# Second attention of a two-layer trunk: TensorE's order written by hand

## The chip, the cores and the metric

One core of one Trainium2 chip runs the whole program. The metric is the device time of one execution in microseconds (us); of the kernel before, three runs took 2441.55, 2447.61 and 2448.34 us, so the median is 2447.61 us.

## The reference

Two decoder layers on 256 tokens of width 2048. The change touches the attention of the second layer, a stick-breaking attention with 16 heads of 128. Cut to what matters:

```python
q, k, v = jnp.split(h @ w_in, 3, axis=-1)          # 2048 -> 3 * 2048
z = jnp.einsum('bqhd,bshd->bhqs', qb, k) * scale
log_beta = jax.nn.log_sigmoid(z)
log_rest = jnp.where(strict, log_beta - z, 0.0)
later = lax.cumsum(log_rest, axis=3, reverse=True) - log_rest
weights = jnp.where(strict, jnp.exp(log_beta + later), 0.0)
o = jnp.einsum('bhqs,bshd->bqhd', weights, v)
y = o @ w_out                                       # 2048 -> 2048
```

## The kernel before

All weights are float32 in HBM. A **unit** of weights (`unit`, L329) is 512 rows by 512 columns: `fetch` (L98) loads it in two halves, ScalarE rounds each half to a high part `whi` and VectorE takes the low part `wlo` (`split`, L127 to L129), and TensorE multiplies both (L123 to L125, or L353 to L355). There are four buffers of each part, so two units can be ready or in use at a time. Each call of `unit` also ticks a **filler** (L310): it sums the adaLN weights of other parts of the model on VectorE (`add_row`, L205) and, at the end of each part, has TensorE do a little work. For a gate that is `gate_end` (L240), two products of a split sum with ones (L244, L245), which VectorE then multiplies into `gg` (L246), and the next quarter of the sum is split into `ahl`, which has one buffer (`gate_split`, L234). For columns it is `ada_columns` (L207), four transposes into `col` (L215) that VectorE sums (L216). A tick does 112/52 = 2.15 steps on the average in this stage (L963), and its steps are written before the unit's own products.

The second attention works on four groups of four heads (`hq` 0 to 3, L1047). `b_project(hq)` (L968) makes q, k and v of a group: four units for each, and it yields after each unit. `b_out(hq)` (L1032) multiplies a group's output with four units of `w_out` and yields after each. `b_attend(hq, pair)` (L997) does two heads, a **pair**: four products for the logits `z` of each head (L1006 to L1009), on ScalarE the absolute values (L1010), an Exp (L1012), a Ln after a table load (L1013), on VectorE `e` (L1015), then on TensorE the sums along the keys (L1016 to L1018), on ScalarE the Exp of the sums after another table load (L1021), and on TensorE the products with v into `bo` (L1024, L1025), which ScalarE and VectorE split into the two parts of `o` (L128, L129). Each sub-step of TensorE with float32 operands shows as two rows of the trace.

PSUM banks are handed out by rings. In this stage:

```python
banks(f=(0, 1), m=(2, 3), z=(4, 5, 7), s=(6,))     # L962
def small_ps(name, tag="s"): return bank(tag, name) # L153
```

The ring `s` has one bank, 6: `bo` of either head, `gate` and `col` all take it, so each waits until the one before it has been read. q and k use `f`, v and the units of `b_out` use `m`.

In which order the instructions of an engine stand is decided when the program is built: a scheduler takes, engine by engine, the earliest written instruction that it reckons ready, so it moves products of the units between the steps of a pair. The order is fixed once the program is built, and each engine works through its own in that order.

Of the kernel before, what the change touches and what calls it, by code (L numbers as in the profile page):

```python
# [12 lines left out]
AF = mybir.ActivationFunctionType  # L13
# [3 lines left out]
P = 128  # L17
# [26 lines left out]
def trunk(ctx: ExitStack, tc: tile.TileContext, x, c, rel_bias, ada_w, ada_b, norm_g, a_w_in, a_q_norm,  # L44
          a_kv_norm, a_idx_k_norm, a_w_qb, a_w_idx_qb, a_w_uk, a_w_uv, a_w_out, b_w_in, b_w_out,
          mlp_w1, mlp_w2, bucket, out):
    nc = tc.nc
# [7 lines left out]
    def uid(prefix, _n=[0]):  # L55
        _n[0] += 1
        return f"{prefix}_{_n[0]}"
# [12 lines left out]
                            fill=0.0, base=0, channel_multiplier=1)  # L70
# [5 lines left out]
                            fill=1.0, base=1 - P, channel_multiplier=1)  # L76
# [7 lines left out]
                            fill=-1.0, base=-1, channel_multiplier=-1)  # L84
# [34 lines left out]
    def rows(w, k0, k1, c0, c1):  # L119
        return w.rearrange("(a p) n -> p a n", p=P)[:, k0:k1, c0:c1]  # L120
# [6 lines left out]
    def split(dst_hi, dst_lo, src):  # L127
        return (nc.scalar.activation(dst_hi, src, AF.Copy).ins,  # L128
                nc.vector.tensor_sub(dst_lo, src, dst_hi.bitcast(F32)).ins)  # L129
# [18 lines left out]
    def bank(kind, name):  # L148
        ring = rings[kind]
        ring[1] += 1  # L150
        return psum.tile([P, BLK], F32, tag=f"bank{ring[0][(ring[1] - 1) % len(ring[0])]}", name=uid(name))

    def small_ps(name, tag="s"):  # L153
        return bank(tag, name)
# [174 lines left out]
    def unit(src, a, n, weight=1, into=None):  # L329
        if prepared:  # L330
            return prepared.pop()
        r = halves(fetch(src, a, n), a, n, into)
        filler.tick(weight)
        return r


    def s_piece(u, xk, nf, ps_tiles, n):

        for f in range(nf):
            o = ps_tiles[f // 2][:, (f % 2) * T:(f % 2 + 1) * T]  # L340
            fs = slice(f * P, (f + 1) * P)
            for k, hi, lo in u:
                xh, xl = xk(k)
                mm3(o, hi[:, fs], lo[:, fs], xh, xl, start=(k == 0 and f % 2 == 0), stop=(k == n - 1))

    def m_piece(u, xk, ps_tiles, n, tiles=range(NT)):

        for t in tiles:
            ts_ = slice(t * P, (t + 1) * P)
            o = ps_tiles[t]  # L350
            for k, hi, lo in u:
                xh, xl = xk(k)
                nc.tensor.matmul(o, xh[:, ts_], hi, start=(k == 0), stop=False)  # L353
                nc.tensor.matmul(o, xl[:, ts_], hi, start=False, stop=False)  # L354
                nc.tensor.matmul(o, xh[:, ts_], lo, start=False, stop=(k == n - 1))  # L355
# [121 lines left out]
    @contextmanager  # L477
    def quiet(what="hold"):

        with tc.issue_after(pace[what][0]), tc.issue_after(pace[what][1]):  # L480
            yield

    def pair_tile(i, name):

        return arena.tile([P, 2, 2, T], F32R, tag=f"slot{i}", name=uid(name))
# [11 lines left out]
    def first_products(ps_tiles, ws):  # L497

        for t in range(NT):
            for k, w in enumerate(ws):  # L500
                nc.tensor.matmul(ps_tiles[t], first32[t, k // 4][:, k % 4], w, start=(k == 0), stop=False)
# [83 lines left out]
    outs = ((pq, BLK, 0), (pk, W2, BLK))  # L585
    waiting = []
    for i in range(len(steps) + LEAD):
        if i < len(steps):
            start_load(i)
            g, k, _ = steps[i]  # L590
# [103 lines left out]
    for u in range(4):  # L694
# [7 lines left out]
        for a in range(2):  # L702
            qi = q_tile[:, u % 2, a].rearrange("p (a t) -> p a t", a=2)
            nc.scalar.activation(qi, pf[a].rearrange("p (a t) -> p a t", a=2), AF.Copy)
            for b in range(2):
# [7 lines left out]
                for t in range(NT):  # L713
                    o = score[:, rng[t][0]]
# [107 lines left out]
    for s in (slice(0, P), slice(2 * P, 3 * P)):  # L822
        nc.gpsimd.affine_select(out=score[:, s], in_=score[:, s], pattern=[[-1, P]], compare_op=ALU.is_ge,
                                fill=SENT, base=0, channel_multiplier=1)
    for t in range(NT):
        o = score[:, rng[t][0]]
# [5 lines left out]
    for s in (slice(0, P), slice(2 * P, 3 * P)):  # L832
        nc.gpsimd.affine_select(out=mask[:, s], in_=mask[:, s], pattern=[[-1, P]], compare_op=ALU.is_ge,
                                fill=-1.0, base=0, channel_multiplier=1)
# [133 lines left out]
    def b_project(hq):  # L968

        res = {}  # L970
        for part, tag in ((2, "v"), (0, "q"), (1, "k")) if hq == 0 else ((0, "q"), (1, "k"), (2, "v")):
            c0 = part * D + hq * BLK
            ps = [bank("m" if tag == "v" else "f", "p" + tag) for _ in range(2)]
            for u in range(4):
                first = hq == 0 and tag == "v"
                if first and u < 2:
                    if u == 0:
                        first_products(ps, early.pop("b"))
                    continue
                with quiet() if first else nullcontext():  # L980
                    prt = unit(rows(b_w_in[0], u * 4, u * 4 + 4, c0, c0 + BLK), 4, BLK)
                w = [(u * 4 + i, hi, lo) for i, (hi, lo) in enumerate(prt)]
                if tag == "v":
                    m_piece(w, hof, ps, NC)
                else:
                    s_piece(w, hof, 4, ps, NC)
                if u < 3:
                    yield
            both = arena.tile([P, 2, BLK], F32, tag=f"slot{12 + 2 * 'vkq'.index(tag) + hq % 2}", name=uid(tag))
            res[tag] = [both[:, i] for i in range(2)]  # L990
            for o, p_ in zip(res[tag], ps):
                nc.scalar.activation(o, p_, AF.Copy, scale=QS if tag == "q" else 1.0)
            yield
        projected[hq] = [[x_.rearrange("p (a t) -> p a t", a=2) for x_ in res["q"]],
                         [x_.rearrange("p (a t) -> p a t", a=2) for x_ in res["k"]], res["v"]]

    def b_attend(hq, pair):  # L997
        qT, kT, vt = projected[hq]
        kw = dict(skip_group_check=True)
        zs = []  # L1000
        both = arena.tile([P, 2, 3 * P], F32, tag=("slot18", "e")[pair[0] // 2], name=uid("e"))
        es = [both[:, i] for i in range(2)]
        for hl in pair:
            q_, k_ = qT[hl // 2][:, hl % 2], kT[hl // 2][:, hl % 2]
            z = small_ps("z", "z")
            nc.tensor.matmul(z[:, :T], k_[:, :P], q_, start=True, stop=False, **kw)  # L1006
            nc.tensor.matmul(z[:, T:3 * P], k_[:, P:], q_[:, P:], start=False, stop=False, **kw)
            nc.tensor.matmul(z[:, :P], big_ident, strict, start=False, stop=False, **kw)
            nc.tensor.matmul(z[:, T:3 * P], big_ident, strict, start=False, stop=True, **kw)  # L1009
            nc.scalar.activation(es[hl % 2], z[:, :3 * P], AF.Abs)  # L1010
            zs.append(z)
        nc.scalar.activation(both, both, AF.Exp, scale=-1.0)  # L1012
        nc.scalar.activation(both, both, AF.Ln, bias=1.0)  # L1013
        for z, e in zip(zs, es):
            nc.vector.scalar_tensor_tensor(e, z[:, :3 * P], 0.0, e, op0=ALU.max, op1=ALU.add)  # L1015
            nc.tensor.matmul(z[:, :T], neg_tri, e[:, :T], start=False, stop=False, **kw)  # L1016
            nc.tensor.matmul(z[:, P:T], neg_ones, e[:, T:], start=False, stop=False, **kw)
            nc.tensor.matmul(z[:, T:3 * P], neg_tri, e[:, T:], start=False, stop=True, **kw)  # L1018
        oo = pair_tile(8 + hq % 2 * 2 + pair[0] // 2, "o")
        for hl, (z, e) in enumerate(zip(zs, es), pair[0]):  # L1020
            nc.scalar.activation(e, z[:, :3 * P], AF.Exp)  # L1021
            po = small_ps("bo")
            hs = slice(hl * P, (hl + 1) * P)
            nc.tensor.matmul(po[:, :T], vt[0][:, hs], e[:, :T], start=True, stop=False, **kw)  # L1024
            nc.tensor.matmul(po[:, P:T], vt[1][:, hs], e[:, T:], start=False, stop=True, **kw)  # L1025
            o = oo[:, hl % 2]
            split(o[:, 0], o[:, 1], po[:, :T])
            o_tiles[hq].append(o)
# [3 lines left out]
    def b_out(hq):  # L1032
        for d in ((0,), (1,), (2,), (3,)) if hq < 3 else ((0,), (1, 2, 3)):
            kw = {}
            if d == (1, 2, 3):
                hts, ahead = next_h(mods[1, 4], mods[1, 3])
                handed.append(hts)
                kw = dict(early=lambda: load_mlp(1), ahead=ahead, hold=(12, 13, 14, 15))
            out_part(b_w_out[0], 4 * hq, 4, o_of(o_tiles[hq]), yt, gates.get((1, 2)), ss, d, hq == 0, hq == 3,
                     ("x", "f", "m")[-len(d):],  # L1040
                     **kw)
            yield

    yt, ss = new_y(ypool)
    for _ in b_project(0):
        pass
    for hq in range(4):  # L1047
        fill = []
        if hq > 0:
            fill.append((b_out(hq - 1), 2))  # L1050
        if hq < 3:
            fill.append((b_project(hq + 1), 6))
        for pair in ((0, 1), (2, 3)):
            b_attend(hq, pair)
            for gen, n in fill:
                for _ in range(n):
                    next(gen)
        for gen, _ in fill:
            for _ in gen:
                pass  # L1060
    filler.finish()
    for _ in b_out(3):
        pass
# [50 lines left out]
```

## Time and profile before

| what | value |
|---|---|
| median of 3 runs | 2447.61 us |
| the profiled execution | 2444.33 us |
| its span, first to last instruction | 2442.5 us |
| TensorE busy | 2350.5 us, 96% of the span |
| VectorE busy | 1747.2 us, 72% |
| ScalarE busy | 1222.3 us, 50% |
| from the first logits of the second attention to the first unit of `b_out(3)` | 1350.6 to 1678.4 us |

Busy time is the union of an engine's instructions. TensorE's products overlap, so one that is held up for a moment leaves less idle time in the trace than it lost; the distance between two starts tells more. The granted clock is given as a share of full speed: 1.00 is 2.4 GHz, 0.50 is 1.2 GHz.

### The profile page before, as it was taken

The numbers are of one execution on the slowest core, as the hardware profiler recorded it, in microseconds if no ns is written. First come the engines' busy times: TensorE is split into PE (matmuls) and PEld (weight loads), VectorE is DVE, ScalarE is ACT, GpSimd is POOL, SyncE is SP. The second block draws the span as 40 slices with busy tenths as digits, with TensorE's granted clock in tenths as the row PEclk, the third lists the DMA queues.
The fourth block names the chain that finished last, engine by engine and source line by source line (L and its number), as shares of the span: only waits on it lengthen the run. The fifth ranks groups of instructions, "written<-read, shape, count | busy, mean of one in ns | idle before, by whom it ended". The sixth has DMA issues, their size and how long they took to land.

```text
span 2442.5 us, 32827 instructions
## 1 busy us (share of the span) xinstructions
PE 2350.5 (96%) x12292; PEld 1957.9 (80%) x12292; DVE 1747.2 (72%) x2218; ACT 1222.3 (50%) x1825; POOL 41.0 (2%) x74
## 2 busy tenths in 40 slices
PE   5789999999999999999999999999999999999998
PEld 2478887868888888888878989987788888888886
DVE  6789798888576876876567678887855557655556
ACT  3056555566544544444455554456654454454443
POOL 0010000000000000000000000000000000000000
PEclk9799999999999999999999999999999999999999
DMA  9986789857677877877657779896666557656554
GB/s 371 346 311 233 267 307 309 292 206 267 232 261 246 293 269 274 303 253 272 193 186 257 239 264 328 304 335 221 235 239 191 185 188 263 216 189 190 182 189 146
DMA packets 281831, 613.93 MB, mean 251 GB/s; under 512 B 19668, under 2 KB 36392, under 8 KB 281160
## 3 DMA queue, kind: packets, MB, share of 16 engines
q1 hardware_dynamic: 278544, 603.14, 71.8%
q0 software_dynamic: 2464, 8.53, 1.2%
q8 instruction: 96, 1.57, 0.3%
q14 instruction: 63, 0.52, 0.1%
q10 hardware_dynamic: 664, 0.17, 0.0%
HBM read 609.62 MB, written 2.15 MB: 250 GB/s over the span
## 4 chain that ended last, share of the span: by engine, by line
PE 78%; DMA 7%; DVE 5%; ACT 4%; issue 4%; POOL 0%; SPq 0%; DVEq 0%; POOLq 0%; ACTq 0%
PE f L884 18%; PE m L355 11%; PE m L354 11%; PE m L353 11%; PE f L886 9%; DVE acc L205 2%; DMA raw<-in_a_w_out_dram 2%; DMA w<-in_ada_w_dram 2%; DMA adaw<-in_ada_w_dram 1%; ACT whi L128 1%; PE pv L353 1%; PE pv L354 1%; PE pv L355 1%; DVE wlo L129 1%; PE pq L123 1%
## 5 line engine op out<-in xcount | busy, mean ns | idle before, releaser
L129 DVE TENSOR_TENSOR wlo<-raw,whi 128x1024 fp32r<-128x1024 f32 x726 | 875.5, 1220 | 424.6 <-ACT whi L128 421.5
L128 ACT ACTIVATE whi<-raw 128x1024 fp32r<-128x1024 f32 x726 | 756.0, 1056 | 806.9 <-PE f L884 311.2
L884 PE MATMUL f<-h,whi 128*128 128x512 f32 x1920 | 675.9, 394 | 0.0
L886 PE MATMUL f<-h,wlo 128*128 128x256 f32 x1920 | 543.2, 283 | 0.2 <-DVE wlo L129 0.2
L884 PEld LDWEIGHTS f<-h,whi 128*128 128x128 f32 x1920 | 360.6, 188 | 82.5
L205 DVE SCALAR_TENSOR_TENSOR acc<-adaw,cs,acc 128x1024 f32<-128x1024 f32 x300 | 384.1, 1280 | 53.1 <-DMA adaw<-in_ada_w_dram 49.8
L353 PE MATMUL m<-whi,hid 128*128 128x512 f32 x1016 | 401.4, 395 | 0.0
L355 PE MATMUL m<-wlo,hid 128*128 128x512 f32 x1016 | 400.9, 395 | 0.0
L354 PE MATMUL m<-whi,hid 128*128 128x512 f32 x1016 | 400.9, 395 | 0.0
L886 PEld LDWEIGHTS f<-h,wlo 128*128 128x128 f32 x1920 | 360.9, 188 | 1.9 <-DVE wlo L129 0.8
L355 PEld LDWEIGHTS m<-wlo,hid 128*128 128x128 f32 x1016 | 191.3, 188 | 44.7
L353 PEld LDWEIGHTS m<-whi,hid 128*128 128x128 f32 x1016 | 191.4, 188 | 44.0
L354 PEld LDWEIGHTS m<-whi,hid 128*128 128x128 f32 x1016 | 191.4, 188 | 43.3
L387 DVE TENSOR_TENSOR y<-m,y 128x512 f32<-128x512 f32 x200 | 136.7, 685 | 38.4 <-PE m L355 38.0
L353 PE MATMUL m<-whi,o 128*128 128x512 f32 x368 | 149.8, 407 | 0.0
L355 PE MATMUL m<-wlo,o 128*128 128x512 f32 x368 | 146.5, 400 | 0.4 <-DVE wlo L129 0.4
L354 PE MATMUL m<-whi,o 128*128 128x512 f32 x368 | 146.8, 399 | 0.0
L205 DVE SCALAR_TENSOR_TENSOR acc<-w,cs,acc 128x1024 f32<-128x1024 f32 (+1 forms) x74 | 79.6, 1075 | 11.1 <-DMA w<-in_ada_w_dram 8.9
L355 PEld LDWEIGHTS m<-wlo,o 128*128 128x128 f32 x368 | 69.4, 189 | 15.6 <-DVE wlo L129 1.0
L353 PEld LDWEIGHTS m<-whi,o 128*128 128x128 f32 x368 | 69.6, 189 | 13.6 <-ACT qkv L754 0.2
L354 PEld LDWEIGHTS m<-whi,o 128*128 128x128 f32 x368 | 69.6, 189 | 13.3
L123 PE MATMUL pk<-h,whi 128*128 128x256 f32 x256 | 72.8, 284 | 0.0
(274 smaller groups left out, 2912.9 us busy)
## 6 DMA issues: line engine op xcount, KB each, us to landing
raw<-in_mlp_w_dram SPq DMA_DIRECT2D x504, 512.0 KB, 4.5
adaw<-in_ada_w_dram SPq DMA_DIRECT2D x320, 512.0 KB, 6.3
raw<-in_b_w_in_dram SPq DMA_DIRECT2D x92, 512.0 KB, 5.2
raw<-in_a_w_out_dram SPq DMA_DIRECT2D x64, 512.0 KB, 5.6
w<-in_ada_w_dram SPq DMA_DIRECT2D x62, 512.0 KB, 10.3
raw<-in_b_w_out_dram SPq DMA_DIRECT2D x32, 512.0 KB, 6.9
raw<-in_a_w_qb_dram SPq DMA_DIRECT2D x16, 512.0 KB, 5.9
win<-in_a_w_in_dram SPq DMA_DIRECT2D x3, 1824.0 KB, 12.0
```

The costliest lines, as they stand in the source:

```text
L123: nc.tensor.matmul(o, sh, mh, start=start, stop=False, skip_group_check=True)
L128: return (nc.scalar.activation(dst_hi, src, AF.Copy).ins, nc.vector.tensor_sub(dst_lo, src, dst_hi.bitcast(F32)).ins)
L129: nc.vector.tensor_sub(dst_lo, src, dst_hi.bitcast(F32)).ins)
L205: nc.vector.scalar_tensor_tensor(acc, w, cs[:, k:k + 1], acc, op0=ALU.mult, op1=ALU.add)
L353: nc.tensor.matmul(o, xh[:, ts_], hi, start=(k == 0), stop=False)
L354: nc.tensor.matmul(o, xl[:, ts_], hi, start=False, stop=False)
L355: nc.tensor.matmul(o, xh[:, ts_], lo, start=False, stop=(k == n - 1))
L387: nc.vector.tensor_add(y, pt[d][t], y)
L884: nc.tensor.matmul(pf[f], hi[:, fs], hb.rearrange("p a t -> p (a t)"), start=(u == 0 and i == 0), stop=False, skip_group_check=True)
L886: nc.tensor.matmul(pf[f][:, :T], lo[:, fs], hb[:, 0], start=False, stop=(u == 3 and i == 3), skip_group_check=True)
```

## The change

TensorE's instructions from the loop over the four groups are put into a block in which TensorE issues them strictly in the order in which they are written (`manual_schedule`); the other engines' orders, and where TensorE's instructions from outside the block fall among them, stay with the scheduler. `b_attend` becomes three steps, with a `yield` after the logits' work up to `e`, and one after the sums and their Exp; the Exp of both heads are written together. Between the steps the loop puts units by hand: `p` is the next unit of `b_project(hq + 1)`, `o` the next of `b_out(hq - 1)`, and a letter whose units are used up does nothing.

```diff
@@ b_attend
             nc.vector.scalar_tensor_tensor(e, z[:, :3 * P], 0.0, e, op0=ALU.max, op1=ALU.add)
+        yield
+        for z, e in zip(zs, es):
             nc.tensor.matmul(z[:, :T], neg_tri, e[:, :T], start=False, stop=False, **kw)
             nc.tensor.matmul(z[:, P:T], neg_ones, e[:, T:], start=False, stop=False, **kw)
             nc.tensor.matmul(z[:, T:3 * P], neg_tri, e[:, T:], start=False, stop=True, **kw)
         oo = pair_tile(8 + hq % 2 * 2 + pair[0] // 2, "o")
+        for z, e in zip(zs, es):
+            nc.scalar.activation(e, z[:, :3 * P], AF.Exp)
+        yield
         for hl, (z, e) in enumerate(zip(zs, es), pair[0]):
-            nc.scalar.activation(e, z[:, :3 * P], AF.Exp)
             po = small_ps("bo")
@@
-    for hq in range(4):
-        fill = []
-        if hq > 0:
-            fill.append((b_out(hq - 1), 2))
-        if hq < 3:
-            fill.append((b_project(hq + 1), 6))
-        for pair in ((0, 1), (2, 3)):
-            b_attend(hq, pair)
-            for gen, n in fill:
-                for _ in range(n):
-                    next(gen)
-        for gen, _ in fill:
-            for _ in gen:
-                pass
+    with tc.manual_schedule(engines={mybir.EngineType.PE}):
+        for hq in range(4):
+            proj = b_project(hq + 1) if hq < 3 else iter(())
+            outs = b_out(hq - 1) if hq > 0 else iter(())
+
+            def units(kinds):
+                for kind in kinds:
+                    next({"p": proj, "o": outs}[kind], None)
+
+            for pair in ((0, 1), (2, 3)):
+                heads = b_attend(hq, pair)
+                next(heads)
+                units("po" if hq < 3 else "o")
+                next(heads)
+                units("pp" if hq < 3 else "o")
+                next(heads, None)
+                units("opp" if pair[0] == 0 else "op")
+            units("p" * 12 + "o" * 4)
     filler.finish()
```

## Rows read from the trace of the kernel before

**Rows 1.** The page's first part: span; busy time and share of TensorE.

```profile
span 2442.5 us, 32827 instructions
PE 2350.5 (96%) x12292; PEld 1957.9 (80%) x12292; DVE 1747.2 (72%) x2218; ACT 1222.3 (50%) x1825; POOL 41.0 (2%) x74
```

**Rows 2.** Stretches: length; busy PE, PEld, DVE, ACT, POOL; PE clock; DMA share; GB/s.

```profile
1304.52:1327.56 23.04, 23.04 (x194) 23.04 (x192) 18.18 (x16) 8.78 (x10) 0.00 (x0) 1.00 0.93 325
1412.95:1435.25 22.30, 22.30 (x99) 18.08 (x98) 15.55 (x16) 10.20 (x12) 0.00 (x0) 1.00 0.95 339
1350.60:1678.40 327.80, 319.57 (x2035) 286.89 (x2033) 247.74 (x263) 172.34 (x215) 1.98 (x4) 0.99 0.83 293
1358.20:1361.60 3.40, 3.40 (x13) 3.04 (x14) 0.24 (x1) 1.63 (x2) 0.00 (x0) 0.50 0.53 204
1401.20:1404.60 3.40, 3.36 (x23) 3.17 (x24) 3.33 (x4) 2.65 (x4) 0.00 (x0) 1.00 0.99 383
```

**Rows 3.** TensorE's waits in that stage: waiter, releaser, us in total, times, longest.

```profile
PE z L1016 <- DVE e L1015: 8.1, 8, 2.4
```

**Rows 4.** Timeline, second pair, logits to sums: start, us, engine, line, [idle before].

```profile
1396.56 1.01 ACT L1010 ACTIVATE e<-z 128x384 f32<-128x384 f32 x2
...
1396.81 0.22 PE L1009 MATMUL z<-strict,big_ident 128*128 128x128 bf16 x1
...
1398.46 1.28 ACT L1013 ACT_TABLE_LOAD   x1
...
1400.63 1.02 DVE L1015 SCALAR_TENSOR_TENSOR e<-z,e 128x384 f32<-128x384 f32 x2 [1.34 <-ACT e L1013]
1401.24 0.70 PE L1016 MATMUL z<-e,neg_tri 128*128 128x256 f32 x2 [1.20 <-DVE e L1015]
```

**Rows 5.** Timeline, first pair, its sums' first product.

```profile
1358.03 1.06 PE L1016 MATMUL z<-e,neg_tri 128*128 128x256 f32 x2 [2.43 <-DVE e L1015]
```

**Rows 6.** The page's groups: line, shapes, count | busy, mean ns | idle before.

```profile
L128 ACT ACTIVATE whi<-raw 128x1024 fp32r<-128x1024 f32 x726 | 756.0, 1056 | 806.9 <-PE f L884 311.2
L205 DVE SCALAR_TENSOR_TENSOR acc<-adaw,cs,acc 128x1024 f32<-128x1024 f32 x300 | 384.1, 1280 | 53.1 <-DMA adaw<-in_ada_w_dram 49.8
```

**Rows 7.** Timeline, third pair, from `bo` of one head to the next.

```profile
1443.11 0.70 PE L1024 MATMUL bo<-e,v 128*128 128x256 f32 x2
...
1443.79 0.47 PE L354 MATMUL m<-whi,o 128*128 128x512 f32 x1
...
1444.07 0.38 ACT L128 ACTIVATE o<-bo 128x256 fp32r<-128x256 f32 x1 [0.27 <-PE bo L1025]
...
1444.48 0.42 DVE L129 TENSOR_TENSOR o<-bo,o 128x256 fp32r<-128x256 f32 x1 [2.83 <-ACT o L128]
...
1445.03 0.63 PE L1024 MATMUL bo<-e,v 128*128 128x256 f32 x2
```

**Rows 8.** Timeline, second pair, the same step where VectorE was busy.

```profile
1403.11 0.70 PE L1024 MATMUL bo<-e,v 128*128 128x256 f32 x2
...
1405.40 0.42 DVE L129 TENSOR_TENSOR o<-bo,o 128x256 fp32r<-128x256 f32 x1
```

**Rows 9.** Timeline, one gate step and the next, with the splits around them.

```profile
1382.87 0.28 PE L244 MATMUL gate<-ahl,ones_r 128*128 128x256 f32 x1
...
1383.67 0.41 ACT L128 ACTIVATE ahl<-acc 128x256 fp32r<-128x256 f32 x1
...
1384.80 0.42 DVE L129 TENSOR_TENSOR ahl<-acc,ahl 128x256 fp32r<-128x256 f32 x1
1385.03 0.36 PE L244 MATMUL gate<-ahl,ones_r 128*128 128x256 f32 x1
```

**Rows 10.** Timeline, two column steps in a row.

```profile
1505.35 0.60 PE L215 MATMUL col<-ident,acc 128*128 128x128 f32 x4
...
1506.15 0.68 DVE L216 TENSOR_REDUCE mod<-col 128x4 f32<-128x512 f32 x1
...
1506.89 0.66 PE L215 MATMUL col<-ident,acc 128*128 128x128 f32 x4
```

## The prediction

> **What bounds the kernel now.** I read the page first: TensorE is busy 96% of the span, so what counts is where it stands still or runs slowly [rows 1]. Next the busy time by stretches. The stage that the change touches lasts 327.8 us, and in it TensorE is busy 319.57, so 8.2 us are idle [rows 2]. Then TensorE's own waits in that stage: one kind alone is listed, the first sum along the keys waiting for `e` of L1015, 8.1 us in 8 waits, one for each pair [rows 3]. DMA, at 0.83 of its share there, ends no wait of TensorE in the stage. So weights come in time, and the whole loss is the chain from a pair's logits to its sums.
>
> The timeline of the second pair shows that chain: absolute values, Exp, 1.28 us of table load, Ln, `e`, and from the last product of the logits at 1396.81 to the first sum at 1401.24 it is 4.4 us, with nothing else in between [rows 4]. The first pair's wait is the longest, 2.43 us [rows 5], and after it the granted clock is 0.50, the lower level, for 3.4 us; after the 1.20 us of the second pair it stayed at 1.00 [rows 2, 4, 5]. Half speed for 3.4 us costs 1.7 us.
>
> Products overlap. One of 256 columns is 0.28 us long, but starts come 0.12 us apart (23.04 us for 192), so a wait costs about 0.16 us more than its listed idle time; 8 times that is 1.3 us. What the stage has to give is therefore 8.2 + 1.3 + 1.7 = 11.2 us, 0.46% of the time. No order of TensorE can bring more, since its products stay the same.
>
> **What the change removes.** Between logits and sums there is now a whole unit (groups 0 and 3) or two (groups 1 and 2). A unit is 23.04 / 4 = 5.76 us of q or k, or 22.30 / 4 = 5.58 us of v or `w_out` [rows 2]. The chain is 4.4 us undisturbed, and with one or two weight splits of 1.06 us put into it on ScalarE [rows 6] 5.5 to 6.5 us. In groups 1 and 2 the cover of 11.3 us is ample; in groups 0 and 3 nothing to 0.9 us can be left in each of four pairs. From the last product of the logits to the first sum these four pairs took 5.9, 4.4, 6.2 and 4.4 us before (the second is shown [rows 4]); I take 0.5 us in all, with a range of 0 to 2. So -11.2 + 0.5 = **-10.7 us**.
>
> **What it adds: the second head's products.** A pair's two `bo` are now written back to back, with nothing between, and both need bank 6. The second must wait until ScalarE and VectorE have read the first. In the third pair, where both engines were free, the first `bo` starts at 1443.11, TensorE's next product at 1443.79, and the second `bo` at 1445.03, 0.12 us after VectorE ended at 1444.90 [rows 7]. The scheduler had five products of a unit in that gap; in the written order it is empty, and costs 1445.03 - 1443.79 = 1.24 us. Where VectorE was in the middle of something else, its part ended at 1405.82, and the same sum gives 1405.94 - 1403.79 = 2.15 us [rows 8]. Over the eight pairs, first `bo` to end of VectorE's part, the sums are 1.2, 2.15, 1.24, 1.94, 1.93, 1.24, 1.44 and 1.24, on average 1.55 (shortest kind and longest are shown [rows 7, 8]). Before, this was covered in every pair. In the new order the first `bo` also falls right behind a unit's end, when ScalarE splits the weights that the freed buffers let in, so the low end is less likely than it was; with a split of 1.06 us on ScalarE and half a step of 1.28 us on VectorE in the way [rows 6] it is 2.9 at most. For the last pair, products of `b_out(3)` from outside the block may fill the gap, so I count 7 of 8: 7 x 1.55 = **10.9 us** (8.7 to 20).
>
> **What it adds: the filler's work on TensorE.** The steps are written ahead of a unit's products, and were free to float before; now they hold up the queue. Ten units of `b_project(0)` tick before the block, and 6 of these bring nothing, so the block's unit r is tick m = r + 4, with floor(112 m / 52) steps done. For the first gate's two halves that puts steps at r = 4 (first quarter), 5 (second and third), 6 (fourth), and 14 (first and second), 15 (third and fourth); for the two column parts at r = 23 (both), 31, 32, 40 (both) and 48 (both).
> Two of these stand directly behind a pair's second `bo` and wait for bank 6 once more: r = 4, which the letters place after the first pair, and r = 40. The same 1.55 each: **3.1 us** (2.5 to 5.8).
> Two gate steps in one tick, three times: the second needs the next `ahl`, which ScalarE can only write after the first's products. From one gate's first product to the next's took 1385.03 - 1382.87 = 2.16 us, with the split's 0.41 and 0.42 behind other work [rows 9]; less 0.23 for its own two products, 1.9. From the durations alone (0.40 to the end of the first gate, 0.41, 0.42, and some 0.2 between them, less the gate's own) about 1.1. I take 1.5: **4.5 us** (3.3 to 5.8).
> Two column steps in one tick, three times: the second waits for VectorE's sum of 0.68 us. 1506.89 - 1505.35 = 1.54, less 0.36 for four transposes, is 1.2, of which 0.2 was VectorE starting late [rows 10]: 1.0 to 2.0, I take 1.2: **3.6 us** (3.0 to 6).
> Nothing waits for weights: the loads are written, and so fetched, in the new order of the units, and VectorE's sums for a tick run ahead of the unit that they are written with. Banks 2 and 3 change hands only where a unit or a pair lies between, or half a unit later. Those terms are nothing; if the scheduler orders VectorE badly against the fixed queue, it shows as waits for `wlo`.
>
> **The clock.** The added waits come in clusters: `bo`, gate, gate in the first group, `bo`, columns, columns at r = 40. A wait of 2.43 us brought the half clock, one of 1.20 did not [rows 2, 4, 5]. I count two falls of 1.7 us: **3.4 us** (none to six, 10 us).
> By the Trainium skill ("TensorE: Matmul & The Clock Gate", section "A second HAM failure mode: psum-queue depth-cycling") frequent short idles between groups of products that cycle through PSUM banks make the clock go back and forth, with no long wait needed. The trace's seven waits of 1.2 us and less, one in some 40 us, don't show it; it speaks against this change, and is a rival below.
>
> **Sum.** -10.7 + 10.9 + 3.1 + 4.5 + 3.6 + 3.4 = **+14.8 us**. On the profiled execution's 2444.33 us that is 2459; it lies 3.3 us below the median of the runs, on which the same sum gives 2462. I say **2460**. Low ends: -11.2 + 8.7 + 2.5 + 3.3 + 3.0 = +6.3, so 2451. High ends: -9.2 + 20 + 5.8 + 5.8 + 6 + 10 = +38, so 2483.
>
> **Rivals.** (a) *The waits are there, but short.* ScalarE and VectorE are free whenever TensorE waits for them, and the clock stays up: the low ends, +6.3, 2451. For it: an engine that waits feeds no new work to the others. Against: five of eight pairs were undisturbed before, but in the middle of a unit, not at its end. 7 us are 0.3%, about what a measurement of this kernel can tell from no change, so this counts as the same.
> (b) *Faster.* The sums' waits go, and what takes their place is filled: -11.2 at best, 2433. The mechanism is bank 6 coming free while TensorE still has written work between two of its users. It decides below 11.2 us of added waits, over 15 places 0.75 us each; the least that any row shows is 1.0. It needs the second `bo` not to wait, and [rows 7] speaks against that.
> (c) *The order is hardly changed.* If the block's order came out near the scheduler's, the time would stay within 2 us, 2444 to 2447. The scheduler did cover the sums in part, but it put products between the two `bo` each time, and the text of the block can't.
> (d) *The clock oscillates.* Each pair's `bo` wait drops the clock for 3.4 us, as the first pair's wait did: eight falls, 13.6 us in place of 3.4, so +25, 2469; with contended waits 2478. The skill's rule just named would bring it.
>
> **How the numbers follow.** Forecast 0.56, (d) 0.18, (a) 0.14, (c) 0.06, (b) 0.06. Slower takes the forecast and (d), 0.74; the same takes (a) and (c), 0.20; faster is (b), 0.06. The range reaches from (a)'s 2449 (2451 less the 2 us by which runs differ from their sum) to (d)'s upper end 2478, and leaves out (b), (c) and the farthest part of the high ends.
>
> **What would show it.** In the profile after: the waits of L1016 for L1015 fall from 8.1 us to under 2. TensorE's waits for `o` of L129 at L1024 rise from next to nothing to some 8 us listed or more, in 7 or 8 waits of 1 to 2.5 us. New waits of L244 for `ahl` or L129, and of L215 for L216, some 6 to 10 us together. The granted clock shows one or more dips in the stage. The stage is then about 343 us long. I am wrong if the second `bo` follows the first within 0.8 us, if waits for `wlo` show, or if the stage is shorter than 328 us.

## The result, and the profile after

The changed kernel takes 2474.0 us (median of 5 runs, 2469.4 to 2479.6) against 2446.2 us before (median of 5, 2441.6 to 2448.3). The ratio is 1.0119, with a 95% interval of 1.0105 to 1.0134: slower by 1.2%, some 28 us. The profiled execution took 2477.1 us, 32.7 us more than the profiled one of before.

The page's first lines, of the kernel after; they answer to [rows 1]:

```profile
span 2475.3 us, 32819 instructions
PE 2361.8 (95%) x12292; PEld 1967.5 (79%) x12292; DVE 1748.3 (71%) x2218; ACT 1221.8 (49%) x1825; POOL 41.2 (2%) x74
```

The same products take 11 us longer on TensorE, and the span grew by three times that: so there is both slower work and more standing still. TensorE's waits in the stage (waiter, releaser, us in total, times, longest), where before there was the one row of [rows 3]:

```profile
PE bo L1029 <- DVE o L129: 17.4, 7, 3.6
PE col L215 <- DVE mod L216: 2.5, 2, 1.7
PE gate L244 <- ACT ahl L128: 1.9, 1, 1.9
PE gate L244 <- ACT whi L128: 1.8, 1, 1.8
PE gate L244 <- DVE gg L246: 1.8, 1, 1.8
PE bo L1029 <- ACT e L1024: 1.1, 1, 1.1
PE z L1019 <- DVE e L1016: 1.0, 2, 0.8
PE col L215 <- DVE o L129: 0.9, 1, 0.9
PE gate L244 <- DVE o L129: 0.9, 1, 0.9
```

The old waits, the sums' for `e` (now L1019 for L1016), fell from 8.1 to 1.0 us. In their place stand the second heads' waits for the reading of the first (`bo`, now L1029), and the filler's. Next the stage by stretches (length; busy PE, PEld, DVE, ACT, POOL; clock; DMA share; GB/s), from the first logits to the first transposes of the next part, before and after, and two stretches of after at the lower clock:

```profile
1350.60:1702.00 351.40, 342.07 (x2130) 304.81 (x2129) 265.56 (x292) 183.63 (x241) 3.09 (x6) 1.00 0.80 285
```

```profile
1351.06:1736.25 385.19, 354.98 (x2131) 315.56 (x2129) 266.73 (x292) 182.95 (x241) 3.09 (x6) 0.96 0.75 260
1418.78:1425.61 6.83, 6.03 (x15) 4.88 (x16) 3.65 (x5) 0.38 (x1) 0.00 (x0) 0.50 0.87 291
1640.65:1650.89 10.24, 7.78 (x22) 6.03 (x23) 4.63 (x9) 0.38 (x1) 0.00 (x0) 0.50 0.47 141
```

The stage is 33.8 us longer, all that the span gained and 1 us more. Idle time is 385.19 - 354.98 = 30.2 us, before 9.3. The clock fell six times in it, for 34.1 us in all, of which TensorE worked 29.9; half of that, 14.9 us, is lost. Before, one fall cost 1.7.

What makes the longest of the waits is in the timeline of the second pair after (start, us, engine, line, [idle before]; weight loads left out):

```profile
1414.32 2.61 DVE L205 SCALAR_TENSOR_TENSOR acc<-adaw,cs,acc 128x1024 f32<-128x1024 f32 x2
...
1414.54 1.06 ACT L128 ACTIVATE whi<-raw 128x1024 fp32r<-128x1024 f32 x1 [1.42 <-PE pk L124]
...
1415.18 0.59 PE L1029 MATMUL bo<-e,v 128*128 128x256 f32 x2
1415.50 0.58 ACT L992 ACTIVATE k<-pk 128x512 f32<-128x512 f32 x1
1415.61 0.38 PE L1030 MATMUL bo<-e,v 128*128 128x128 f32 x2
1415.98 1.05 ACT L128 ACTIVATE whi<-raw 128x1024 fp32r<-128x1024 f32 x1
1416.84 2.35 DVE L129 TENSOR_TENSOR wlo<-raw,whi 128x1024 fp32r<-128x1024 f32 x2
1416.93 0.37 ACT L128 ACTIVATE o<-bo 128x256 fp32r<-128x256 f32 x1
...
1419.11 0.42 DVE L129 TENSOR_TENSOR o<-bo,o 128x256 fp32r<-128x256 f32 x1
...
1419.58 1.22 PE L1029 MATMUL bo<-e,v 128*128 128x256 f32 x2 [3.59 <-DVE o L129]
```

The first head's products stand right behind a unit that finished k. Its end lets ScalarE copy k and split the weights of a later unit, and both come ahead of the reading of `bo` on ScalarE; on VectorE two of the filler's sums (L205, until 1416.84) and both low parts do. The reading ends at 1419.53, not at the 1416.9 that it would have reached with nothing ahead of it (1.69 us after the start of `bo`, as in the run with the reading first, below). From 1415.18 to 1419.58 are 4.40 us; a pair's first `bo` alone holds TensorE 0.57 (1374.03 to 1374.60 in the run without the block, below), so 3.83 are lost. In the third pair [rows 7] the same step took 1.24.

The sixth pair stands behind a k unit too, with the same copy of k in ScalarE's queue, but with no sum of the filler on VectorE:

```profile
1638.35 1.23 DVE L129 TENSOR_TENSOR wlo<-raw,whi 128x1024 fp32r<-128x1024 f32 x1 [3.33 <-ACT whi L128]
1639.78 1.23 DVE L129 TENSOR_TENSOR wlo<-raw,whi 128x1024 fp32r<-128x1024 f32 x1 [0.20 <-ACT whi L128]
1640.92 0.42 DVE L129 TENSOR_TENSOR o<-bo,o 128x256 fp32r<-128x256 f32 x1
```

Its loss is 2.93 us (1637.89 to 1641.39, less 0.57). The filler's sums are thus good for some 0.9 of the 3.83.

### The profile page after: what moved, and what is told of

Its sections match the earlier page's. It is cut to its first block, busy times and chain, and to the rows that moved or that the text cites. A ratio compares the mean times of both kernels' runs of the same rounds, so it can differ in the third digit from the quotient of the medians.

```text
span 2475.3 us, 32819 instructions
## 1 busy us (share of the span) xinstructions
PE 2361.8 (95%) x12292; PEld 1967.5 (79%) x12292; DVE 1748.3 (71%) x2218; ACT 1221.8 (49%) x1825; POOL 41.2 (2%) x74
## 4 chain that ended last, share of the span: by engine, by line
PE 78%; DMA 8%; DVE 6%; issue 4%; ACT 3%; POOL 0%; SPq 0%; DVEq 0%; POOLq 0%; ACTq 0%
PE f L884 17%; PE m L353 12%; PE m L355 12%; PE m L354 12%; PE f L886 9%; DMA w<-in_ada_w_dram 2%; DMA adaw<-in_ada_w_dram 2%; DVE acc L205 2%; DVE wlo L129 2%; DMA raw<-in_a_w_out_dram 1%; ACT whi L128 1%; PE pv L353 1%; PE pv L354 1%; PE pv L355 1%; PE pq L123 1%
## 5 line engine op out<-in xcount | busy, mean ns | idle before, releaser
L129 DVE TENSOR_TENSOR wlo<-raw,whi 128x1024 fp32r<-128x1024 f32 x726 | 875.6, 1221 | 458.4 <-ACT whi L128 455.3
L205 DVE SCALAR_TENSOR_TENSOR acc<-adaw,cs,acc 128x1024 f32<-128x1024 f32 x300 | 384.3, 1281 | 55.6 <-DMA adaw<-in_ada_w_dram 52.6
L205 DVE SCALAR_TENSOR_TENSOR acc<-w,cs,acc 128x1024 f32<-128x1024 f32 (+1 forms) x74 | 79.6, 1075 | 11.5 <-DMA w<-in_ada_w_dram 9.3
```

What stands on the lines that cost most here:

```text
L205: nc.vector.scalar_tensor_tensor(acc, w, cs[:, k:k + 1], acc, op0=ALU.mult, op1=ALU.add)
```

## The experiments

The theory was that two things make the loss, both with the half clock that follows: the one bank for both heads, made worse by its place right behind a unit, and the filler's steps in TensorE's fixed queue. The main rivals were that the written order costs time by itself, whatever the bank, and that loads, splits and sums now come in a worse order. Each run was compared with the kernel before on the same chip.

**A second bank for the heads.** Block and letters stay:

```diff
-    banks(f=(0, 1), m=(2, 3), z=(4, 5, 7), s=(6,))
+    banks(f=(0, 1), m=(2, 3), z=(4, 5), s=(6,), o=(7, 6))
...
-            po = small_ps("bo")
+            po = small_ps("bo", "o")
```

> The changed kernel with one edit: the logits keep banks 4 and 5, and the two heads' products with v take banks 7 and 6 in turn, so the second need not wait for the first to be read. Theory (the second head waits for the one bank, and these waits bring most of the half clock): the seven waits of the second head, 19 us together, go, and with them some 8 us of half clock; the gate and column steps still wait for bank 6. About 2474 - 25 = 2449 us (2443 to 2456). Rival (the written order itself is the cost, because each wait in it holds up all of TensorE, and without this wait another, for the weights or the filler, ends in its place): the time stays above 2465 us.

Measured: 2454.5 us, ratio to before 1.0046 (1.0031 to 1.0062). That is 1.0119 - 1.0046 = 0.73% of the time, 18 us, given back by one bank. The waits of the second head for the first are gone from TensorE's list; what is left of the new ones is the filler's, and those for the sums and the last Exp. The waits of L215 for `mod` and of L244 for `ahl`, `whi` and `gg` are as long as after the change; the others:

```profile
PE col L215 <- DVE o L129: 2.4, 1, 2.4
PE bo L1029 <- ACT e L1024: 2.3, 1, 2.3
PE gate L244 <- DVE o L129: 2.1, 1, 2.1
PE z L1019 <- DVE e L1016: 1.9, 2, 1.2
```

The theory's direction holds; the time came out above the 2449 us, near the upper end. The two waits for `o` of L129 grew from 0.9 to 2.1 and 2.4 us, since the filler's step behind the second head now arrives earlier and meets the same queue, and the last pair's wait for its Exp grew from 1.1 to 2.3, 3.9 us together.

**No block.** The three steps and the letters stay, the scheduler orders TensorE again:

```diff
-    with tc.manual_schedule(engines={mybir.EngineType.PE}):
+    if True:
```

> The changed kernel without the block: the three steps and the letters stay as they are written, but the scheduler orders TensorE again. Theory (the loss comes from TensorE holding strictly to the written order): the scheduler again puts products of the units between the two heads and around the filler's steps, and the time is near the kernel before, 2446 us (2441 to 2452), with waits for the sums of some us left. Rival (the loss comes from the order in which loads, splits and steps are written, whatever TensorE does): above 2460 us.

Measured: 2436.2 us, ratio 0.9968 (0.9954 to 0.9982): faster than the kernel before by 0.3%, and below the 2441 to 2452 of the theory, which expected no difference. The order in which things are written is thus a gain, and the block alone turns it into a loss of some 37 us. TensorE's timeline, first pair of this kernel:

```profile
1374.03 0.59 PE L1029 MATMUL bo<-e,v 128*128 128x256 f32 x2
1374.46 0.38 PE L1030 MATMUL bo<-e,v 128*128 128x128 f32 x2
1374.60 0.36 PE L123 MATMUL pq<-h,whi 128*128 128x256 f32 x1
...
1377.23 0.70 PE L1029 MATMUL bo<-e,v 128*128 128x256 f32 x2
```

The two heads' products stand as far apart as after the change (3.2 us in the first pair both times), but the scheduler has put 21 products of the next unit between them. The sums' waits are what the letters aimed at, and they are gone here too: 0.9 us in one wait.

**A unit between the two heads.** One bank, block kept:

```diff
+            if hl % 2:
+                yield
             po = small_ps("bo")
...
                 next(heads, None)
-                units("opp" if pair[0] == 0 else "op")
+                units("o" if hq == 3 or (hq > 0 and pair[0] > 0) else "p")
+                next(heads, None)
+                units("op" if pair[0] == 0 and hq < 3 else "p" if hq > 0 else "")
```

> The changed kernel with one unit of the letters written between the two heads' products with v, on one bank as before; only the last pair has none. Theory: a unit is 5.6 to 5.8 us and the longest wait of the second head 3.8 us, so the waits go with the one bank kept, and so does most of the half clock that they bring: 2449 us (2442 to 2457). In the second head's place the first gate and column steps may now wait. Rival (the bank's reading is not what holds the second head, but its own operands): the waits stay, above 2465 us.

Measured: 2455.7 us, ratio 1.0052 (1.0035 to 1.0068). The second heads' waits for the reading are gone here as well, with the bank as it was. So it is the missing work between the heads, not the bank as such. The filler's steps behind a head wait more, 5.1 us for two gates and 3.0 for a column step, as the edit puts them behind the first head and the second.

**The reading ahead of the splits.** The unit whose splits fall on the first head's reading is held behind it on both engines:

```diff
...
+                    if n == 1:
+                        with tc.issue_after(first_o[1]), tc.issue_after(first_o[2]):
+                            made = next(gen, 0)
...
```

(`first_o` holds the two instructions that read the pair's first `bo`, `n` counts the units since. What is held is all that the two engines do for that unit, its filler's sums included.)

> The changed kernel with one edit: the weight splits of the second unit after a pair's products with v, which fall just when the first head's output is to be read, are put behind that reading on ScalarE and VectorE. Theory (the waits of the second head are 1.3 to 3.8 us long, and not 1.2, because the reading queues behind the two splits of a unit): they fall to 1.2 to 2.2 us each, some 10 us in place of 19, and half of the half clock goes: about 2460 us (2452 to 2466). Rival (reading simply takes that long there, or VectorE's sums for the filler are what is in the way): no change, above 2468 us.

Measured: 2463.6 us, ratio 1.0087 (1.0067 to 1.0108). The row of the wait, and the same place as shown above of after:

```profile
PE bo L1029 <- DVE o L129: 6.5, 7, 0.9
```

```profile
1418.54 0.59 PE L1029 MATMUL bo<-e,v 128*128 128x256 f32 x2
...
1419.39 0.38 ACT L128 ACTIVATE o<-bo 128x256 fp32r<-128x256 f32 x1
1419.68 2.00 ACT L128 ACTIVATE whi<-raw 128x1024 fp32r<-128x1024 f32 x2
1419.81 0.42 DVE L129 TENSOR_TENSOR o<-bo,o 128x256 fp32r<-128x256 f32 x1 [4.15 <-ACT o L128]
...
1420.29 0.70 PE L1029 MATMUL bo<-e,v 128*128 128x256 f32 x2 [0.93 <-DVE o L129]
```

17.4 us of waits became 6.5, and all seven are 0.93 us. From start to start are now 1.75 us, the shortest of any run with one bank and nothing between; the 1.24 us lost of [rows 7] was this floor (here 1.18). Everything above it was the queue on ScalarE and VectorE. The edit moves splits and filler's sums together, so it does not part the theory from the rival's second half; the pairs of the profile after do, as shown above: both take part, and the sums the smaller one. Half of the gain went again: the other waits of the stage grew from 11.9 to 17.3 us, among them the filler's steps behind the second head, from 0.9 to 2.3 us each.

**One of the filler's steps on TensorE for a tick.** One bank, block kept:

```diff
+            ended = False
             while self.due >= 1.0:
+                ends = self.done < self.limit and self.steps[self.done][3] >= NC
+                if self.single and ended and ends:
+                    break
+                ended = ended or ends
                 self.due -= 1.0
...
```

(`ends` is true for a step that works on TensorE; `single` is set for this stage.)

> The changed kernel with one edit: in this stage a tick does at most one of the filler's steps on TensorE, and leaves the rest to the next unit. One bank for the two heads is kept. Theory (two such steps in one tick cost about 1.9 us each time on TensorE and bring a half clock of their own): three gate waits and two column waits, 9 us together, go, but a moved column step now falls behind a second head and waits for bank 6 for 1.2 us; with two or three of the six falls of the clock gone, 4 to 5 us: about 2474 - 12 = 2462 us (2456 to 2467). Rival (the clock falls come from the second head's waits alone, and the filler's waits only fill time that the weights would take anyway): 2470 us or more.

Measured: 2467.1 us, ratio 1.0101 (1.0086 to 1.0116). A smaller gain than expected, between the theory's range and the rival's bound. Its waits say why:

```profile
PE bo L1036 <- DVE o L129: 17.3, 7, 4.2
PE gate L244 <- DVE o L129: 2.7, 2, 1.7
PE col L215 <- DVE o L129: 1.9, 2, 0.9
PE bo L1036 <- ACT e L1031: 1.7, 1, 1.7
```

The waits for `ahl`, `whi`, `gg` and `mod` are gone, 8 us of them. But two of the moved steps, not one, landed right behind a second head, and the clock did not recover: 26.9 us of work at the lower clock, against 29.9. All five falls of this run came with a second head's wait, which it leaves as it was; but near four of them a step of the filler waits behind that head, so what the heads' waits bring alone is not shown.

**Both edits.** The second bank (here 7 and 4, so that bank 6 is the filler's alone), and one step for a tick; block and letters kept.

> The changed kernel, block and letters kept, with both causes taken away: the two heads take banks 7 and 4 in turn, so neither waits for the other nor the filler for them, and a tick does at most one of the filler's steps on TensorE. Theory (these two, and the half clock that they bring, are the whole loss): what stays are the last pair's wait for its Exp and one or two waits for sums, 3 to 4 us together, so the time is below the kernel before by some 8 us: 2436 us (2431 to 2441). Rival (there is a third cost of the written order, in the weights' order or in the engines' orders around it): 2445 us or more.

Measured: 2431.5 us, ratio 0.9949 (0.9936 to 0.9962): faster than the kernel before by 0.5%, and the fastest of all runs. The stage, and all of TensorE's waits in it and just behind it:

```profile
1351.20:1691.88 340.68, 337.59 (x2131) 303.64 (x2129) 265.65 (x293) 182.87 (x241) 3.08 (x6) 1.00 0.83 295
```

```profile
PE hT L455 <- ACT xn L452: 3.5, 2, 2.7
PE bo L1036 <- ACT e L1031: 1.4, 1, 1.4
PE z L1026 <- DVE e L1023: 0.6, 1, 0.6
PE m L361 <- DVE wlo L129: 0.3, 1, 0.3
```

(The first row belongs to the part that follows; it was 3.8 us before and 3.5 after.) Idle time is 3.1 us, the clock never falls. No third cost of the written order shows.

**The bank alone in the kernel before**, and **the letters with banks 7 and 4 but no block**:

> The kernel before with the bank edit alone: logits on banks 4 and 5, the two heads' products with v on 7 and 6. Theory: before, the scheduler filled the time in which the bank is read, so a second bank gains nothing: within 3 us of the kernel before. Rival (banks bring time by themselves, whatever the order): 8 us or more below the kernel before.

Measured: 2444.4 us, ratio 1.0002 (0.9991 to 1.0013). No difference, as expected.

> The changed kernel without the block, letters kept, and with the heads' products with v on banks 7 and 4. Without the block alone the run had 2436.2 us against 2443.3 before, with some 1.3 us left of waits of the second head and 1.2 of a gate. Theory: the second bank takes the former away and changes nothing else: 2435 us (2431 to 2439), the same as without it within what can be told. Rival (the scheduler's order shifts as a whole with the banks, and the gain of the letters was luck of one order): 2443 us or more.

Measured: 2435.7 us, ratio 0.9968 (0.9958 to 0.9979), the same as without the bank. Where the scheduler fills the reading, the second bank is worth nothing; in the block it is worth 18 us.

**One sum for all of them.** From each run's trace: the stage's length, idle time (length less busy time), waits over 0.25 us, the time that TensorE worked at the lower clock, and what is left when idle time, 0.16 us for each wait (the overlap of products that the prediction names) and half of the slow time are taken off.

| kernel | stage us | idle | waits | worked at half clock | left |
|---|---|---|---|---|---|
| before | 351.4 | 9.3 | 9 | 3.4 | 338.9 |
| after | 385.2 | 30.2 | 17 | 29.9 | 337.3 |
| second bank | 364.2 | 17.5 | 11 | 15.9 | 337.0 |
| one step for a tick | 377.1 | 24.7 | 14 | 26.9 | 336.7 |
| both | 340.7 | 3.1 | 4 | 0 | 337.0 |
| no block | 346.4 | 6.5 | 8 | 0 | 338.6 |
| unit between | 364.5 | 18.8 | 12 | 12.5 | 337.6 |
| reading first | 374.5 | 24.6 | 18 | 19.1 | 337.5 |
| bank alone, before | 353.2 | 10.2 | 10 | 3.0 | 339.8 |
| letters, banks, no block | 343.1 | 4.5 | 4 | 0 | 338.0 |

What is left agrees within 3.1 us, while the stages differ by 45: waits and clock explain every difference but for these 3 us, and within the kernels with the block (336.7 to 337.6) all but 1. Each row is one execution; that of one step for a tick took 4.7 us more than the median of its runs, that of the reading first 7.3 more.

## Why the prediction was right or wrong, point by point

It said slower, by waits for bank 6 and by the filler's steps, and by +14.8 us. The way and the places were right; the size was half of what came, 28 us in the medians.

- **What the stage has to give, 11.2 us:** right. With both causes removed the runs gained 0.5%, 12 us.
- **The sums' waits, 0.5 us left:** near. Two waits of 1.0 us together, 1.3 with the overlap.
- **The second head, 10.9 us:** the place right, the size wrong, 19.1. By the distances from the first `bo` to the second, less 0.57, the seven waits cost 2.63, 3.83, 1.85, 3.83, 2.69, 2.93 and 1.30, which is 19.1 us. The step that failed is the price of 1.55 taken from [rows 7, 8]. Those places were in the middle of a unit, where the scheduler had put them; the prediction saw that the new place is behind a unit's end, and yet took the old mean, with the new place for an upper end only. It put one split of ScalarE and half a step of VectorE in the way; the profile after shows both low parts of a unit, 2.35 us on VectorE, in four of the seven waits, and in the second and fourth pair, 3.83, sums of the filler ahead of the low parts. The copy of k in ScalarE's queue adds little: the sixth pair has it too, and lost 2.93, the fifth without it 2.69. So even the upper end, 2.9, was too low for two pairs. The run with the reading first shows the floor at 1.18 and the queue as the rest.
- **Bank 6 behind the second head, 3.1 us:** two waits of 0.93 listed, 2.4 us. Right.
- **Gates, 4.5 us:** three waits where they were expected. From start to start less 0.23 they are 1.9, 1.9 and 2.1, 6.0 us in all: the disturbed price of [rows 9], not a value between that and the floor.
- **Columns, 3.6 us:** two waits, 2.0 and 1.2 us. The third place had none, since the last step of all fell to the `finish` behind the block.
- **The last pair:** not foreseen. With no unit left between its sums and its products with v, TensorE waits 1.1 us for the Exp.
- **The clock, 3.4 us:** the second term that failed, 14.9 us. The count of two falls came from clusters that were seen; there were six, and two lasted twice and one three times as long as the fall of before. The prediction priced its added waits and the clock apart. In the table above they mostly grow together, from 3.1 us idle and no fall to 30.2 and 29.9; yet two kernels with 24.6 and 24.7 us idle worked 19.1 and 26.9 us at the lower clock, so the idle time alone does not set it. Its rival (d) had the price nearly right (13.6 us of it) with the wrong picture, one fall for each pair, so that agreement is luck; four of the six falls came with a second head's wait (in two of these a step of the filler followed at once), and two behind a gate's.
- **Weights:** right. No wait for `wlo` shows in the stage.

Where the 33.8 us of the stage come from: idle time +20.9, overlap at the waits' ends +1.3, clock +13.2, and 1.6 less in what is left. Added up as measured, the prediction's terms with the last pair's come to some +37 us; the 3 us above the stage's are not traced. The rival (a), short waits and no fall of the clock, fell with the queue behind the units; (b) and (c) with the waits that the profile shows. What is open: which of the waits brings which fall. The runs change waits and falls together, and five executions of the changed kernel took 2469 to 2480 us at mean clocks of 0.982 to 0.985, so falls differ from one execution to the next.

## What to carry to other kernels

An order written by hand must have work between any two steps that share one buffer, for as long as its reading takes at that very place; a unit's end, where freed buffers let a burst of splits in, was a bad place here to ask another engine for something quick. Price a wait in the place where the new order puts it, behind what will be queued there, not by what the old order shows of it. Small side work with steps of its own on the engine belongs in the count: here it floated under the scheduler and blocked in the fixed queue. And when idle time is put into a busy matrix engine, count the lower clock that may follow with it: 20.9 us more idle time came with 13.2 us more by the clock.

## What the runs showed of the hardware

A wait's length does not tell by itself whether the clock falls. In the profile after, listed waits of 1.76 us were followed by the lower clock twice, at 1388.1 and 1456.3, each about 1.3 us after the wait had ended, while waits of 1.90 (at 1466.6) and 2.45 us (at 1594.0) were not. Three falls lasted 3.4 us, as in [rows 2], two 6.8 and one 10.2; the longest was the cluster of three waits at 1640, whose row stands above. The first of the two waits of 1.76 us, and the stretch behind it:

```profile
1386.75 0.35 PE L244 MATMUL gate<-ahl,ones_r 128*128 128x256 f32 x1 [1.76 <-ACT whi L128]
```

```profile
1388.06:1391.48 3.41, 3.41 (x19) 3.41 (x18) 3.31 (x6) 0.00 (x0) 0.00 (x0) 0.50 0.81 257
```

The rule that the prediction weighed, of the Trainium skill ("TensorE: Matmul & The Clock Gate", section "A second HAM failure mode: psum-queue depth-cycling"), is that short idles between groups of products make the clock go back and forth. The trace agrees in part: after the change it does go back and forth, six times, 34 us. But the short idles alone did not do it: with the reading first, five of the seven 0.93 us waits have no fall near them, and the other two stand in clusters with a wait of 2.3 us, that of a gate or column step behind the second head.
